# Norm sums from GpSimd to VectorE, and the root of the FFN norm at a fixed place among TensorE's products

## The chip, the cores and the metric

One core of a Trainium2 chip runs the whole kernel in one launch. The metric is the device time of an execution in microseconds (us). TensorE is called PE in the profile, its weight loads PEld, VectorE DVE, ScalarE ACT, GpSimd POOL, and SP the queue that issues most loads.

## The reference

A decoder trunk of two layers on x of 256 positions and 1024 features, in float32. Each layer is x = x + attention(rmsnorm(x)) @ w_o, then x = x + conv_ffn(rmsnorm(x)); a last rmsnorm follows. What matters here is the norm and the FFN:

```python
def rmsnorm(x, g):
    y = x * lax.rsqrt(jnp.mean(x * x, axis=-1, keepdims=True) + RMS_EPS)
    return y * g

def conv_ffn(h, w_up, conv_w, conv_b, w_down):      # h 256x1024, w_up 1024x5632, w_down 2816x1024
    u = h @ w_up
    up = jnp.pad(u, ((0, 0), (2, 0), (0, 0)))
    c = conv_b
    for j in range(3):
        c = c + conv_w[j] * up[:, j:j + S]
    val, gate = jnp.split(c, 2, axis=-1)
    return (jax.nn.silu(gate) * val) @ w_down
```

The attention of layer 0 has MoBA and indexer-selected heads, that of layer 1 sixteen dilated-window heads; their projections take the normed x too.

## The kernel before, in words

x is held transposed in xT: 128 partitions of features by 8 blocks k by 256 positions. Every float32 product is made of three products of rounded parts (mm3, line 125): a factor is split into a high part h (ScalarE copy to the rounded type) and a low part l (the difference, on VectorE), and h*h, h*l and l*h are added up in PSUM. Weights are split so by split (line 114), x by split_x (line 201) into xh and xl with the norm's gain g in it. The factor 1/rms of a position isn't needed before the products: it is multiplied in when the result leaves PSUM (in the FFN the tile rb at line 517; in layer 1's projections q_evac, k_evac and r at line 312).

The norm is built by the class Norm (line 208). At the end of an output projection (out_proj, line 413) or of FFN 0 (line 549) TensorE finishes the sum of x in four quarters b, each two blocks k. For each, take adds it to xT on VectorE (line 219), measure squares it on ScalarE (line 227, tile sq) and split_x makes two xh and two xl. In measure the squares of the quarters are added on GpSimd: two additions of 128x512 for b = 1 and 2, and 128x256 ones for b = 2 and 3. After the fourth, two products with a column of ones (line 239, tile sp) sum over the partitions, rsqrt_mean (line 174) makes the mean on VectorE and the power -0.5 on GpSimd, and row_bcast (line 181) spreads the root over the partitions: the root's two parts are multiplied into diagonals (tile d) on VectorE, two products with ones give the tile bp, and ScalarE copies it to rb. All of measure has high priority with the planner.

The FFN (ffn, line 471) runs over 22 steps f. A step loads columns of w_up (a load serves two steps; three buffers raw), splits the value half i = 0 and the gate half i = 1, and makes 24 products for each into one PSUM tile; the tile's tag goes lg, pt, lg, av from step to step, and sp and bp use av too. Then the result is multiplied by rb (u), convolved (c), gated (sg) and split into g. The down products of a step are made three steps later (LAG). The order of an engine's instructions is set when the program is built, by a planner that simulates the engines and takes, of what is ready, the earliest traced or the one with high priority. `behind(gate)` and `tc.issue_after` queue an instruction behind a named one on its engine; `pin` (`tc.keep_in_program_order`) queues it behind the one traced just before it on its engine. The splits of steps 1 to 3 are queued behind the norm's last xh and xl (norm.gate).

In FFN 1 the planner also places 16 transposes of xT to the token layout on TensorE (line 544) and four copies of them on VectorE (line 545). In layer 1 the low part of the first split of the k projection, k_0l, is made on GpSimd (line 758).

Of the kernel before, what the change touches and what calls it, by code (L numbers as in the profile page):

```python
# [34 lines left out]
def trunk(ctx, tc, x, w_in_even, idx_k_norm, w_in_odd, w_o, rel_bias, attn_norm, ffn_norm,  # L35
# [78 lines left out]
    def split(view, shape, name, gate=None, low=nc.vector):  # L114
        with behind(gate):
            return split_now(view, shape, name, low)

    def split_now(view, shape, name, low):
        h = wp.tile([P] + shape, F32R, tag="wh", name=name + "h", bufs=5)
        l = wp.tile([P] + shape, F32R, tag="wl", name=name + "l", bufs=5)  # L120
        nc.scalar.activation(h, view, AF.Copy)  # L121
        low.tensor_tensor(l, view, h.bitcast(F32), ALU.subtract)
        return h, l
# [11 lines left out]

    gps = lg_tile("gps")
# [37 lines left out]
    def rsqrt_mean(ss, n, name, w=2):  # L174
        var = tp.tile([P, w], F32, tag="var", name=name + "v")
        nc.vector.tensor_scalar(var, ss, 1.0 / n, EPS, op0=ALU.mult, op1=ALU.add)
        r = tp.tile([P, w], F32, tag="rstd", name=name + "r")
        nc.gpsimd.tensor_tensor(r, var, mhalf[:, 0:w], ALU.pow)
        return r

    def row_bcast(r, name):
# [5 lines left out]
        ps = av_tile(name + "bp")  # L187
        for i, part in enumerate((rh.bitcast(F32), rl)):
            for t in range(2):
                nc.vector.tensor_scalar(dg[:, i, t, :], ident, part[:, t:t + 1], None, op0=ALU.mult)  # L190
            nc.tensor.matmul(ps[:, 0:S], ones_r, dg[:, i, :, :].rearrange("p t c -> p (t c)"),
                             start=i == 0, stop=i == 1)
        rb = tp.tile([P, S], F32, tag="rb", name=name + "b")
        nc.scalar.activation(rb, ps[:, 0:S], AF.Copy)
        return rb

# [11 lines left out]
    class Norm:  # L208


        def __init__(self, grow, name):
            self.grow, self.name = grow, name

        def take(self, b, acc):
# [10 lines left out]
        def measure(self, b, xv):  # L225
            sq = tp.tile([P, 2, S], F32, tag=("c", "c", "u", "c")[b], name=f"{self.name}sq{b}", bufs=(3, 3, 2, 3)[b])
            nc.scalar.activation(sq, xv, AF.Square)
# [6 lines left out]
            self.sq = sq  # L234
            if b < 3:
                return
# [7 lines left out]
    pin = tc.keep_in_program_order  # L244
# [45 lines left out]
    def proj_fm(w2d, c0, xh, xl, evac, name, gate=(None, None), low=(nc.vector, nc.vector)):  # L290
        raw = load_cols(w2d, c0, name)
        ps = acc_tile(f"{name}p")
        for i in range(2):
            h, l = split(raw[:, :, i * P:(i + 1) * P], [8, P], f"{name}_{i}", gate[i], low[i])
# [176 lines left out]
    def ffn(layer, norm, name, nxt, also=None):  # L471
# [22 lines left out]
        def up(f, raws):  # L494
            ps = rot[f % 4](f"{name}u{f}")
            hl = [split(raws[i][:, :, (f % 2) * P:(f % 2 + 1) * P], [8, P], f"{name}w{f}_{i}",
                        norm.gate if 1 <= f < 4 else None) for i in range(2)]
# [312 lines left out]
```

## Time and profile before

| | us |
|---|---|
| median of 3 runs | 653.55 |
| lowest and highest | 653.11, 653.69 |
| the profiled execution | 653.59 |
| its span | 651.8 |
| PE busy in it | 637.5 |
| DVE busy | 529.9 |
| ACT busy | 406.0 |
| POOL busy | 58.7 |

The span runs from the first to the last instruction on the core; 1.8 us of the profiled execution lie around it. The granted clock was 0.998 of full speed over the span. A timeline line gives start, duration, engine, line of the kernel, operation, out<-in, and in brackets how long the engine had been idle and what released it. Lines of equal kind that follow each other are merged (x4), and their duration runs from the first start to the last end. Names leave out numbers: f0u is any step's result in FFN 0, f0w_0h the high part of its value half's weights.

### The profile page before, as it was taken

The page shows a single profiled execution, that of the slowest core. Times are in us where ns is not written, and L with a number is a line of the kernel's source. Part 1 is how long each engine was busy: PE and PEld are TensorE (multiplying, and loading weights), DVE is VectorE, ACT ScalarE, POOL GpSimd, SP SyncE. Part 2 cuts the span into 40 slices and gives each one's busy share as a digit, 9 for nine tenths or more (in the row PEclk, how much of TensorE's full clock was granted, in tenths as well). Part 3 has the DMA queues.
Part 4 walks back from the last instruction along what each step waited for, and adds up shares of the span by engine and source line. Part 5 has one row for each costly group of instructions (what it writes and reads, how often), then busy time and mean ns, then how long its engine had stood idle before and what let it go on. Part 6 is the DMA issues. An engine that isn't in the chain of part 4 may idle for free.

```text
span 651.8 us, 12933 instructions
## 1 busy us (share of the span) xinstructions
PE 637.5 (98%) x5145; PEld 612.5 (94%) x5145; DVE 529.9 (81%) x1012; ACT 406.0 (62%) x710; POOL 58.7 (9%) x68
## 2 busy tenths in 40 slices
PE   8999999999999999999999999999999999999995
PEld 6999999998999999999989999999999999999994
DVE  6999999968898778877779977865899877777774
ACT  6766775765766555555546866855486555555553
POOL 0100002803000000000013111000300000000002
PEclk9999999999999999999999999999999999999999
DMA  9987645462767666666424533637456655555201
GB/s 276 294 238 189 190 130 194 169 220 90 235 212 220 203 207 211 211 210 210 130 66 133 192 129 132 240 96 247 155 189 222 210 183 183 184 180 185 91 1 64
DMA packets 91604, 116.01 MB, mean 178 GB/s; under 512 B 3447, under 2 KB 83191, under 8 KB 91544
## 3 DMA queue, kind: packets, MB, share of 16 engines
q1 hardware_dynamic: 86492, 110.09, 51.5%
q10 hardware_dynamic: 5052, 5.10, 3.5%
q8 instruction: 40, 0.66, 0.4%
q14 instruction: 20, 0.16, 0.1%
HBM read 113.35 MB, written 1.84 MB: 177 GB/s over the span
## 4 chain that ended last, share of the span: by engine, by line
PE 94%; DVE 3%; DMA 1%; issue 1%; ACT 0%; SPq 0%; POOL 0%; POOLq 0%; DVEq 0%
PE f0u L130 19%; PE f1u L130 19%; PE f1o L130 9%; PE f0o L130 9%; PE a1o L130 3%; PE a0o L130 3%; PE a_0pt L386 1%; PE a1av L395 1%; PE a0av L395 1%; DVE xT L219 1%; PE v12p L130 1%; PE qi1p L130 1%; PE q00p L130 1%; PE v01p L130 1%; PE qi2p L130 1%; PE q12p L130 1%
## 5 line engine op out<-in xcount | busy, mean ns | idle before, releaser
L130 PE MATMUL f0u<-f0xl,f0w_0h 128*128 128x256 f32 x176 | 49.5, 281 | 1.2 <-DVE f0xl L204 1.2
L130 PE MATMUL f1u<-f1xl,f1w_0h 128*128 128x256 f32 x176 | 49.6, 282 | 0.7 <-DVE f1xl L204 0.7
L130 PE MATMUL f0u<-f0xh,f0w_0l 128*128 128x256 f32 x176 | 49.2, 280 | 0.0
L130 PE MATMUL f1u<-f1xl,f1w_1h 128*128 128x256 f32 x176 | 49.2, 280 | 0.0
L130 PE MATMUL f1u<-f1xh,f1w_0l 128*128 128x256 f32 x176 | 49.2, 279 | 0.0
L130 PE MATMUL f1u<-f1xh,f1w_1h 128*128 128x256 f32 x176 | 49.1, 279 | 0.0
L130 PE MATMUL f0u<-f0xl,f0w_1h 128*128 128x256 f32 x176 | 49.1, 279 | 0.0
L130 PE MATMUL f0u<-f0xh,f0w_1l 128*128 128x256 f32 x176 | 49.1, 279 | 0.0
L130 PE MATMUL f0u<-f0xh,f0w_1h 128*128 128x256 f32 x176 | 49.1, 279 | 0.0
L130 PE MATMUL f0u<-f0xh,f0w_0h 128*128 128x256 f32 x176 | 49.1, 279 | 0.0
L130 PE MATMUL f1u<-f1xh,f1w_1l 128*128 128x256 f32 x176 | 49.1, 279 | 0.0
L130 PE MATMUL f1u<-f1xh,f1w_0h 128*128 128x256 f32 x176 | 49.1, 280 | 0.0
L524 DVE SCALAR_TENSOR_TENSOR f1c<-f1us,cv,f1c 128x255 f32<-128x255 f32 (+1 forms) x88 | 36.9, 479 | 0.7 <-ACT f1c L521 0.7
L121 ACT ACTIVATE f1w_0h<-f1uv 128x1024 fp32r<-128x1024 f32 x22 | 23.2, 1056 | 22.2 <-PE f1u L130 20.4
L524 DVE SCALAR_TENSOR_TENSOR f0c<-f0us,cv,f0c 128x255 f32<-128x255 f32 (+1 forms) x88 | 36.9, 477 | 0.0
L121 ACT ACTIVATE f0w_0h<-f0uv 128x1024 fp32r<-128x1024 f32 x22 | 23.3, 1058 | 21.5 <-PE f0u L130 21.5
L130 PEld LDWEIGHTS f1u<-f1xl,f1w_0h 128*128 128x128 f32 x176 | 33.1, 188 | 1.9 <-DVE f1xl L204 1.1
L130 PEld LDWEIGHTS f0u<-f0xl,f0w_0h 128*128 128x128 f32 x176 | 33.1, 188 | 1.8 <-DVE f0xl L204 1.8
L121 ACT ACTIVATE f0w_1h<-f0ug 128x1024 fp32r<-128x1024 f32 x22 | 23.3, 1060 | 17.5 <-PE f0o L130 12.2
L121 ACT ACTIVATE f1w_1h<-f1ug 128x1024 fp32r<-128x1024 f32 x22 | 23.3, 1060 | 16.8 <-PE f1o L130 8.9
L130 PEld LDWEIGHTS f1u<-f1xh,f1w_0h 128*128 128x128 f32 x176 | 33.0, 188 | 0.8
L130 PEld LDWEIGHTS f1u<-f1xh,f1w_0l 128*128 128x128 f32 x176 | 33.1, 188 | 0.0
(1047 smaller groups left out, 2492.3 us busy)
## 6 DMA issues: line engine op xcount, KB each, us to landing
f0dn<-in_w_down_dram SPq DMA_DIRECT2D x11, 1024.0 KB, 4.9
f0uv<-in_w_up_dram SPq DMA_DIRECT2D x11, 1024.0 KB, 6.3
f0ug<-in_w_up_dram SPq DMA_DIRECT2D x11, 1024.0 KB, 6.3
f1dn<-in_w_down_dram SPq DMA_DIRECT2D x11, 1024.0 KB, 5.0
f1uv<-in_w_up_dram SPq DMA_DIRECT2D x11, 1024.0 KB, 6.8
f1ug<-in_w_up_dram SPq DMA_DIRECT2D x11, 1024.0 KB, 5.2
q<-in_w_in_even_dram SPq DMA_DIRECT2D x4, 1024.0 KB, 6.7
k<-in_w_in_even_dram SPq DMA_DIRECT2D x4, 1024.0 KB, 5.9
```

The source lines that it names most:

```text
L121: nc.scalar.activation(h, view, AF.Copy)
L130: m = nc.tensor.matmul(ps, w, a, start=start and i == 0, stop=stop and i == 2, **kw)
L219: nc.vector.tensor_tensor(xv[:, i, :], acc[:, i * S:(i + 1) * S], xv[:, i, :], ALU.add)
L386: m = nc.tensor.transpose(pt[:, c * P:(c + 1) * P], pr[:, c * P:(c + 1) * P], ident)
L395: m = nc.tensor.matmul(o[s * HD:(s + 1) * HD], V[:, t, vc], pts[s][:, qc], start=t == 0, stop=t == 1)
L524: nc.vector.scalar_tensor_tensor(c[:, i, sh:S], u[:, i, 0:S - sh], cv[:, j, col:col + 1], c[:, i, sh:S], op0=ALU.mult, op1=ALU.add)
```

## The change

The additions of the squares leave measure. take keeps the four tiles of squares, and after the fourth quarter sums makes four additions on VectorE, queued behind the last xl and with high priority: a += b, c += d, a += c (128x512 each) and the two halves of a (128x256). The second of them is called half, the fourth sum.

In the FFN the first three steps' products are traced before step 0's result is evacuated. The root (sp, mean, power) is pinned on TensorE between the value half and the gate half of step 1. The diagonals are traced in step 2, and the products that spread the root (over_rows) are pinned between the halves of step 2. On VectorE the low parts of the splits are queued: step 1's two behind half and behind sum, step 2's behind the mean and behind the last diagonal, step 3's behind the last diagonal; their high parts on ScalarE stay behind the last xh.

Layer 1's norm n1 has the same four sums on VectorE, and its root and broadcast are traced by the new measure after the FFN, with high priority as before. The argument low goes away: k_0l is made on VectorE, and k_0's two parts are queued behind the high and low part of the last g of FFN 0.

```diff
-    def split(view, shape, name, gate=None, low=nc.vector):
+    def split(view, shape, name, gate=None):
...
-        low.tensor_tensor(l, view, h.bitcast(F32), ALU.subtract)
+            nc.vector.tensor_tensor(l, view, h.bitcast(F32), ALU.subtract)
...
+            sq = tp.tile([P, 2, S], F32, tag=("c", "c", "u", "c")[b], name=f"{self.name}sq{b}", bufs=(3, 3, 2, 3)[b])
             with tc.high_priority():
-                self.measure(b, xv)
+                nc.scalar.activation(sq, xv, AF.Square)
+            self.sq.append(sq)
             for k in (2 * b, 2 * b + 1):
                 self.gate = split_x(self.xh, self.xl, self.grow, k)
...
-            if b in (1, 2):
-                nc.gpsimd.tensor_tensor(sq, sq, self.sq, ALU.add)
-            if b >= 2:
-                nc.gpsimd.tensor_tensor(sq[:, 0, :], sq[:, 0, :], sq[:, 1, :], ALU.add)
             if b == 3:
-                nc.gpsimd.tensor_tensor(sq[:, 0, :], sq[:, 0, :], self.sq[:, 0, :], ALU.add)
+                self.sums()
+
+        def sums(self):
+
+            a, b, c, d = self.sq
+            with tc.high_priority(), tc.issue_after(self.gate[1].ins):
+                nc.vector.tensor_tensor(a, a, b, ALU.add)
+                self.half = nc.vector.tensor_tensor(c, c, d, ALU.add)
+                nc.vector.tensor_tensor(a, a, c, ALU.add)
+                self.sum = nc.vector.tensor_tensor(a[:, 0, :], a[:, 0, :], a[:, 1, :], ALU.add)
+
+        def root(self, first=lambda m: m):
             ps = av_tile(self.name + "sp")
             for t in range(2):
-                nc.tensor.matmul(ps[:, t:t + 1], sq[:, 0, t * P:(t + 1) * P], ones[:, 0:1], start=True, stop=True)
-            self.r = rsqrt_mean(ps[:, 0:2], D, self.name)
-            self.rb = row_bcast(self.r, self.name)
+                first(nc.tensor.matmul(ps[:, t:t + 1], self.sq[0][:, 0, t * P:(t + 1) * P], ones[:, 0:1],
+                                       start=True, stop=True))
+            self.r, self.mean = rsqrt_mean(ps[:, 0:2], D, self.name)
+
+        def measure(self):
+            with tc.high_priority():
+                self.root()
+                self.rb = row_bcast(self.r, self.name)
...
+            def part(i, behind=None):
+                return split(raws[i][:, :, (f % 2) * P:(f % 2 + 1) * P], [8, P], f"{name}w{f}_{i}",
+                             behind and (norm.gate[0], behind))
+
+            ps = rot[f % 4](f"{name}u{f}")
+            if f == 1:
+                hl = [part(0, norm.half), part(1, norm.sum)]
+            elif f == 2:
+                hl = [part(0, norm.mean)]
+                dg, last_dg = row_diagonals(norm.r, norm.name)
+                hl.append(part(1, last_dg))
+                norm.last = last_dg
+            else:
+                hl = [part(i, norm.last if f == 3 else None) for i in range(2)]
...
+                    if i == 0 and f == 1:
+                        norm.root(pin)
+                    if i == 0 and f == 2:
+                        norm.rb = over_rows(dg, norm.name, pin)
+            return ps
+
+        raws = None
+        ups = [up(f) for f in range(3)]
+        rbb = norm.rb[:, None, :].to_broadcast([P, 2, S])
+        for f in range(NF):
+            ps = ups[f] if f < 3 else up(f)
...
         if not last:
+            nxt.behind = (high, low)
...
+    n1.measure()
     r1, rb1 = n1.r, n1.rb
...
-        gate, low = (n1.gate, nc.gpsimd) if c == 0 else (None, nc.vector)
+        gate, early = (n1.gate, n1.behind) if c == 0 else (None, None)
...
-                (None, gate), (low, nc.vector))
+                (early, gate))
```

## Rows read from the trace of the kernel before

**Rows 1.** The page's first part: busy time, share of the span and instructions of each engine.

```profile
PE 637.5 (98%) x5145; PEld 612.5 (94%) x5145; DVE 529.9 (81%) x1012; ACT 406.0 (62%) x710; POOL 58.7 (9%) x68
```

**Rows 2.** Windows. Columns: the stretch, its length, then busy time and instructions of PE, PEld, DVE, ACT and POOL, granted clock, DMA share, GB/s; a window counts an instruction that reaches into it from the stretch before. First the steady stretch of FFN 0; then its first step's products alone (tile f0u: PE, PEld, DVE); the hold in FFN 0's last products; the first q and the first k projection of layer 1 alone (tiles q10p, k10p); FFN 1's first step, its products alone (line 130: PE, PEld) and its transposes alone (line 544).

```profile
170.00:335.00 165.00, 165.00 (x1417) 165.00 (x1416) 136.06 (x213) 98.54 (x147) 0.00 (x0) 1.00 0.60 192
...
153.65:157.80 4.15, 2.92 (x18) 2.34 (x19) 0.00 (x0) 1.00 0.00 0
...
337.74:339.56 1.82, 0.28 (x3) 0.07 (x2) 1.76 (x1) 0.00 (x0) 1.48 (x1) 1.00 1.05 366
...
343.05:349.86 6.81, 4.71 (x25) 3.50 (x25) 0.00 (x0) 1.00 0.01 2
...
343.05:349.86 6.81, 4.10 (x22) 3.29 (x22) 0.00 (x0) 1.00 0.01 2
...
456.12:461.38 5.26, 3.59 (x21) 2.58 (x20) 1.00 0.25 100
...
456.12:461.38 5.26, 2.67 (x16) 1.86 (x16) 1.00 0.25 100
```

**Rows 3.** The waits of PE: instruction that waited, releaser, us in total, times, longest.

```profile
PE f0o L130 <- DVE f0g L534: 1.5, 1, 1.5
...
PE f0u L130 <- DVE f0xl L204: 1.2, 2, 0.8
...
PE q10p L130 <- DVE n1xl L204: 0.7, 2, 0.4
```

**Rows 4.** Timeline of POOL and then of DVE at FFN 0's norm.

```profile
152.96 2.71 POOL L229 TENSOR_TENSOR f0sq<-f0sq,f0sq 128x512 f32<-128x512 f32 x2 [21.73 <-ACT f0sq L227]
...
152.07 0.48 DVE L204 SCALAR_TENSOR_TENSOR f0xl<-xT,gT,f0xh 128x256 fp32r<-128x256 f32 x1
...
153.24 2.71 DVE L204 SCALAR_TENSOR_TENSOR f0xl<-xT,gT,f0xh 128x256 fp32r<-128x256 f32 x2
155.87 0.74 DVE L219 TENSOR_TENSOR xT<-a0o,xT 128x256 f32<-128x256 f32 x2
156.54 2.14 DVE L204 SCALAR_TENSOR_TENSOR f0xl<-xT,gT,f0xh 128x256 fp32r<-128x256 f32 x4
```

**Rows 5.** Timeline of ACT at the same norm: a square, then the high parts of x.

```profile
153.59 0.62 ACT L227 ACTIVATE f0sq<-xT 128x512 f32<-128x512 f32 x1
154.11 0.49 ACT L203 ACTIVATE f0xh<-xT,gT 128x256 fp32r<-128x256 f32 x1
156.32 0.51 ACT L203 ACTIVATE f0xh<-xT,gT 128x256 fp32r<-128x256 f32 x1 [1.71 <-DVE xT L219]
```

**Rows 6.** Timeline from FFN 0's last g to layer 1's norm: DVE, ACT and POOL.

```profile
335.16 0.42 DVE L528 TENSOR_TENSOR f0sg<-f0sg,f0c 128x256 f32<-128x256 f32 x1
337.12 2.38 DVE L534 TENSOR_TENSOR f0g<-f0sg,f0g 128x256 fp32r<-128x256 f32 x1 [1.54 <-ACT f0g L531]
340.45 1.46 DVE L219 TENSOR_TENSOR xT<-f0o,xT 128x256 f32<-128x256 f32 x4 [0.94 <-PE f0o L130]
...
345.58 3.89 DVE L204 SCALAR_TENSOR_TENSOR n1xl<-xT,gT,n1xh 128x256 fp32r<-128x256 f32 x5
...
336.69 0.40 ACT L531 ACTIVATE f0g<-f0sg 128x256 fp32r<-128x256 f32 x1
...
336.86 2.36 POOL L122 TENSOR_TENSOR k_0l<-k,k_0h 128x1024 fp32r<-128x1024 f32 x1 [172.82 <-ACT k_0h L121]
343.41 2.72 POOL L229 TENSOR_TENSOR n1sq<-n1sq,n1sq 128x512 f32<-128x512 f32 x2 [4.18 <-ACT n1sq L227]
```

**Rows 7.** Timeline of DVE at FFN 1's norm: low parts of x, and the first copy to the token layout.

```profile
455.71 2.79 DVE L204 SCALAR_TENSOR_TENSOR f1xl<-xT,gT,f1xh 128x256 fp32r<-128x256 f32 x2
...
459.48 0.68 DVE L545 COPY f1xtok<-f1xt 128x512 f32<-128x512 f32 x1
460.08 1.78 DVE L204 SCALAR_TENSOR_TENSOR f1xl<-xT,gT,f1xh 128x256 fp32r<-128x256 f32 x2
```

**Rows 8.** Groups of DVE by shape in 170 to 335 us: busy us, mean ns, then idle time before.

```profile
L122 DVE TENSOR_TENSOR f0w_1l<-f0ug,f0w_1h 128x1024 fp32r<-128x1024 f32 x19 | 23.2, 1223 | 0.4 <-ACT f0w_1h L121 0.4
...
L534 DVE TENSOR_TENSOR f0g<-f0sg,f0g 128x256 fp32r<-128x256 f32 x21 | 8.8, 420 | 0.0
```

**Rows 9.** Timeline of the root in FFN 0: PE, POOL and DVE (f0rl reads f0rh; the diagonals f0d are the last).

```profile
161.54 0.50 PE L239 MATMUL f0sp<-ones,f0sq 128*128 128x1 f32 x4
...
163.34 0.70 POOL L178 TENSOR_TENSOR f0r<-f0v,mhalf 128x2 f32<-128x2 f32 x1 [2.37 <-DVE f0v L176]
...
164.07 0.17 DVE L183 CAST f0rh<-f0r 128x2 fp32r<-128x2 f32 x1 [0.81 <-POOL f0r L178]
164.28 0.16 DVE L185 TENSOR_TENSOR f0rl<-f0r,f0rh 128x2 f32<-128x2 f32 x1
...
164.75 0.48 DVE L190 TENSOR_SCALAR f0d<-ident,f0rl 128x128 fp32r<-128x128 f32 x2
```

**Rows 10.** Timeline of SP's queue and of ACT: the load of step 2's gate columns and the split that takes it.

```profile
160.40 0.37 SPq L94 DMA_DIRECT2D f0ug<-in_w_up_dram  x1
...
165.56 1.06 ACT L121 ACTIVATE f0w_1h<-f0ug 128x1024 fp32r<-128x1024 f32 x1 [4.97 <-DMA f0ug<-in_w_up_dram]
```

**Rows 11.** Timeline of DVE and PE at the first down products of FFN 0.

```profile
181.29 0.41 DVE L534 TENSOR_TENSOR f0g<-f0sg,f0g 128x256 fp32r<-128x256 f32 x1
...
181.52 0.63 PE L130 MATMUL f0o<-f0g,f0d0h 128*128 128x256 f32 x4
```

More of the change, by code (lines that the diff above doesn't have):

```diff
@@ L112, in behind @@
             yield
-    def split(view, shape, name, gate=None, low=nc.vector):
+    def split(view, shape, name, gate=None):
         with behind(gate):
[L116 to L121, printed above, removed]
-        low.tensor_tensor(l, view, h.bitcast(F32), ALU.subtract)
+            h = wp.tile([P] + shape, F32R, tag="wh", name=name + "h", bufs=5)
+            l = wp.tile([P] + shape, F32R, tag="wl", name=name + "l", bufs=5)
+            nc.scalar.activation(h, view, AF.Copy)
+            nc.vector.tensor_tensor(l, view, h.bitcast(F32), ALU.subtract)
         return h, l
@@ L133, in mm3 @@
         return m.ins
+    pin = tc.keep_in_program_order
     gps = lg_tile("gps")
@@ L186, in row_bcast, with over_rows @@
         dg = tp.tile([P, 2, 2, P], F32R, tag="dg", name=name + "d", bufs=1)
-        ps = av_tile(name + "bp")
         for i, part in enumerate((rh.bitcast(F32), rl)):
             for t in range(2):
-                nc.vector.tensor_scalar(dg[:, i, t, :], ident, part[:, t:t + 1], None, op0=ALU.mult)
-            nc.tensor.matmul(ps[:, 0:S], ones_r, dg[:, i, :, :].rearrange("p t c -> p (t c)"),
-                             start=i == 0, stop=i == 1)
+                m = nc.vector.tensor_scalar(dg[:, i, t, :], ident, part[:, t:t + 1], None, op0=ALU.mult)
+        return dg, m
+    def over_rows(dg, name, first=lambda m: m):
+        ps = av_tile(name + "bp")
+        for i in range(2):
+            first(nc.tensor.matmul(ps[:, 0:S], ones_r, dg[:, i, :, :].rearrange("p t c -> p (t c)"),
+                                   start=i == 0, stop=i == 1))
         rb = tp.tile([P, S], F32, tag="rb", name=name + "b")
@@ L195, in row_bcast @@
         return rb
+    def row_bcast(r, name):
+        return over_rows(row_diagonals(r, name)[0], name)
     def norm_tiles(name):
@@ L211, in __init__ @@
         def __init__(self, grow, name):
-            self.grow, self.name = grow, name
+            self.grow, self.name, self.sq = grow, name, []
         def take(self, b, acc):
@@ L286, in trunk, with proj_fm @@
                                          start=n + k + i == 0, stop=n == 2 and k == KT - 1, skip_group_check=True))
-    def proj_fm(w2d, c0, xh, xl, evac, name, gate=(None, None), low=(nc.vector, nc.vector)):
+    def proj_fm(w2d, c0, xh, xl, evac, name, gate=(None, None)):
         raw = load_cols(w2d, c0, name)
@@ L293, in proj_fm @@
         for i in range(2):
-            h, l = split(raw[:, :, i * P:(i + 1) * P], [8, P], f"{name}_{i}", gate[i], low[i])
+            h, l = split(raw[:, :, i * P:(i + 1) * P], [8, P], f"{name}_{i}", gate[i])
             for k in range(KT):
@@ L492, in down, with up @@
                         down_tok(f, t, c, h, l, gh, gl)
[L494 to L497, printed above, removed]
-            for ks in (range(0, 6), range(6, 8)) if f == 0 else (range(8),):
-                for i in range(2):
-                    h, l = hl[i]
-                    for k in ks:
-                        mm3(ps[:, i * S:(i + 1) * S], h[:, k, :], l[:, k, :], xh[:, k, :], xl[:, k, :],
-                            k == 0 and i == 0, k == KT - 1, skip_group_check=True)
-            return ps
-        rbb = norm.rb[:, None, :].to_broadcast([P, 2, S])
-        for f in range(NF):
+        def up(f):
+            nonlocal raws
             if f % 2 == 0:
@@ L514, in ffn @@
                     dn.append(raw_dn[:, i, :])
-            ps = up(f, raws)
+            def part(i, behind=None):
[11 more added lines that the diff above has]
+                hl = [part(i, norm.last if f == 3 else None) for i in range(2)]
+            for ks in (range(0, 6), range(6, 8)) if f == 0 else (range(8),):
+                for i in range(2):
+                    h, l = hl[i]
+                    for k in ks:
+                        mm3(ps[:, i * S:(i + 1) * S], h[:, k, :], l[:, k, :], xh[:, k, :], xl[:, k, :],
+                            k == 0 and i == 0, k == KT - 1, skip_group_check=True)
+                    if i == 0 and f == 1:
[8 more added lines that the diff above has]
+            ps = ups[f] if f < 3 else up(f)
             u = tp.tile([P, 2, S], F32, tag="u", name=f"{name}us{f}")
@@ L533, in ffn @@
                 also(f, high.ins)
-            nc.vector.tensor_tensor(gl, sg, gh.bitcast(F32), ALU.subtract)
+            low = nc.vector.tensor_tensor(gl, sg, gh.bitcast(F32), ALU.subtract)
             pend.append((f, gh, gl))
@@ L602, in trunk @@
         nc.vector.tensor_add(ss0s, ss0[:, :, 0], ss0[:, :, 1])
[L603 removed]
+        r0, _ = rsqrt_mean(ss0s, D, "n0")
     kiw = cp.tile([80, S], F32, tag="kiw", name="kiw")
```

16 lines of the change are left out of this document (4 added, 12 removed).

## The prediction

> **What bounds the kernel now.** The order in which I read: the busy shares, the windows of TensorE, its waits, then the timelines of the other engines where it waits. TensorE is busy for 98% of the span [rows 1]. In the long steady stretch of the first FFN it does 1417 products in 165.00 us, 0.1164 us each, without a gap [rows 2]; there nothing but its own work counts, and neither VectorE's 81% nor ScalarE's 62% is a bound. So the change can bring only what TensorE loses at the three norms. The PE waits name the culprit each time as VectorE: the low halves of x (f0xl, n1xl), and once the low half of the last gated value (f0g) [rows 3].
>
> How much is lost is read from stretches against that pace [rows 2]. First step of FFN 0: 18 products take 4.15 us in place of 2.10, loss 2.05. The hold inside f0's last products: 1.82 us for one product, loss 1.70. First step of layer 1's projections: 24 + 22 products (the 25th of the q row begins at the window's end) take 6.81 in place of 5.36, loss 1.45. First step of FFN 1: 18 products (2.10) and 16 transposes, whose weight loads take 1.86 together, fill 3.96 of 5.26, loss 1.30; the loads overlap, so it may be more, and I take 1.40. All four: 6.60 us.
>
> Why is VectorE late? One f0xl takes 0.48 us, but two of them, begun just after GpSimd began its pair of 128x512 additions, take 2.71, and four more take 2.14 under the next ones [rows 4]. The same in layer 1 (three n1xl and two more: 5 in 3.89 against GpSimd's 343.41 onward) and in FFN 1 (2.79 for two, 1.78 for two [rows 6, 7]). And f0g's low half, 0.42 us by its 21 sisters [rows 8], takes 2.38 while GpSimd makes k_0l from 336.86 [rows 6]. Each stretched instruction reads two SBUF operands beside a GpSimd instruction that reads SBUF.
>
> **The change, part by part.** *Removed from GpSimd:* per norm the 128x512 and 128x256 additions, and once the subtraction k_0l. With them the stretching goes, and what TensorE then waits for is ScalarE's and VectorE's plain chain. For FFN 0: two x additions of about 0.42 take 0.74 [rows 4], so queued independent instructions overlap by some 0.08, and one adds 0.40 for an f0xl. VectorE does two f0xl from 153.24 in 0.8 and the last quarter's two x additions in 0.67, so f0xl 4 and 5 end near 155.2 and 155.6. TensorE wants them at 153.65 + 13 x 0.1164 = 155.2 and 155.5. Loss left: about 0.15 of 2.05. ScalarE is no later than that: its xh 5 runs at 154.11, and only the late addition kept xh 6 until 156.32 [rows 5]; two xh of 0.4 and a square of 0.5 by their starts, so from 154.5 it needs 0.4 + 0.5 + 0.5, so xh 7 ends near 156.0 and f0xl 7 near 156.4. In layer 1 f0g's low half comes within 0.5 us of its high half, which need no longer stand behind k_0h (the multiply ends 335.6, f0g high began only at 336.69 [rows 6]); TensorE reaches it at 337.86, so all 1.70 come back. The x chain of that norm starts 1.7 earlier than 340.45 [rows 6], with ScalarE's 1.3 us per quarter as above; the 12 products per quarter of two interleaved projections take 1.4, so nothing is left of the 1.45. In FFN 1 I leave 0.05.
>
> *Added to VectorE:* four sums behind the last xl. No row has a 128x512 addition of two SBUF operands; the neighbours are 0.42 for 128x256 and 1.22 for 128x1024 [rows 8], between them 0.69. A dependent instruction starts 0.21 after one of 0.17 [rows 9], so it waits for the end; an independent one overlaps by 0.08. Sum: 0.61 + 0.73 + 0.73 + 0.34 = 2.4 us. The Trainium skill speaks against such a chain (VectorE: DVE Perf Modes, "The TRN2 errata"): SBUF latency is paid between instructions, and an fp32 tensor_tensor of N elements takes (N+151) cycles at 0.96 GHz. That is an estimate of 2.5 us for the four; by it the sum below would change by 0.05. The trace agrees at both ends (0.42 and 1.22 are what it gives).
>
> What the sums delay is the second step's first split, f1w_0l in FFN 0. Its products begin at 153.65 + 48 x 0.1164 + 0.15 = 159.4 and want the low half 0.23 later. If the planner lets the split in right behind the second sum, it ends at 156.4 + 1.2 + 1.2 = 158.8 and nothing waits; if all four sums (they have high priority) come first, it ends at 160.0 and TensorE waits 0.4. The code allows both; I take the middle, 0.2. In FFN 1 the sixteen transposes give TensorE 1.8 us of other work, but four copies of 0.6 us to the token layout run on VectorE (0.68 with its tail [rows 7]); with two of them ahead of the sums the split ends between 462.7 and 463.8, wanted at 463.6: I take 0.1, and 1.2 if all four copies go first. In layer 1 the splits k_1, v_0, v_1 stand behind the sums, but are wanted only 8.4 us after the start; k_0l, 1.2 us on VectorE after f0g's low half, fits into the 2.2 us from 336.5 to the first x addition, 338.75. Cost 0; if that cover were gone, each would cost its 1.2 or 2.4.
>
> *Moved:* the root. Its two products stand pinned between the halves of step 2, the broadcast between the halves of step 3. They are the same instructions as before (4 passes from 161.54 [rows 9]), so TensorE's work is unchanged. From the root's products the mean is there some 0.7 us later, then the split f2w_0l queued behind it (1.2), GpSimd's power (0.70 [rows 9]), six small VectorE instructions (164.07 to 165.23, 1.2 [rows 9]): the broadcast's diagonals are ready some 3.9 us after the root, and TensorE asks for them 0.36 + 2.8 + 2.8 = 6.0 us after it. f2w_0l itself is wanted at 3.4 and ready at 2.0, or 2.7 if the power stretches it. Cover 0.7 at the least. The Trainium skill (SBUF — State Buffer, "Who interferes with whom") says that of two such instructions the later one blocks for the whole of the other. By that the power and f2w_0l now meet in each FFN where before VectorE stood idle; the stall would be one of the two numbers just used, and both stay inside the cover.
>
> *Queues:* SP's next weight load waits for step 2's first split to free its buffer (issued 160.40, and ScalarE takes it at 165.56 after 4.97 idle [rows 10]). It now goes out near 159.4 and lands near 164.6; its split is done by 167.5, TensorE wants it near 168.7. It moves with the rest, cover about 1 us. In FFN 1 it is the same with about 1 us.
>
> *Later evacuation:* the broadcast now comes at the middle of step 3 of TensorE, so step 1's result is evacuated at about the same absolute time as before while TensorE is 2 us further on. It has three PSUM tiles free of that (steps 2 to 4) and the down products only join when g is there: f0d0's first at 181.52 beside g's low half of 181.29 [rows 11], in the middle of step 5. I cost it at nothing, the cover being steps 4 and 5.
>
> Sum: 6.60 - 0.15 - 0.2 - 0.05 - 0.1 = 6.1 us. The profiled execution took 653.59 us (span 651.8, 1.8 around it, unchanged), 0.04 above the median 653.55: 653.6 - 6.1 = **647.5 us**.
>
> **Rivals.**
> *The sums become the last wait.* The planner puts all sums and FFN 1's copies ahead of the splits: 0.4 in FFN 0, 1.2 in FFN 1 and some of the x chain (0.5) again: 648.6 to 650.5, likeliest 649. For it: high priority on the sums; against it: the split may follow the second sum.
> *The planner's order changes elsewhere.* Layer 1's attention fills TensorE without loss now, so a new order there can only lose; one wait of 0.5 per head pair over eight pairs would be 4: 650.5 to 652.
> *It doesn't do what it says.* If f0xl were long for another reason than GpSimd, only the hold of 1.70 comes back: 651.9; with the sums in the chain ahead of the splits (0.4 to 1.2 twice), up to 653.5. Against it: the same instruction takes 0.48 with GpSimd idle [rows 4].
> *Slower.* The later evacuation decides: if the planner puts f0d0's products right behind step 4 (ending near 176.7) while g is not there before 181, TensorE's queue stands for up to 4.3 us in each FFN: 653.6 - 6.1 + 8.6 = 656. It turns slower once each hold is over 3.05 us. Against it: the planner now waits with d0 until g is there, to 0.2 us [rows 11].
>
> **How the numbers follow.** Forecast (646.2 to 648.6) 0.62; sums last 0.18; order elsewhere 0.08; not as said 0.06, a third of it under 652.2; slower 0.06. The low end is all 6.60 back and 0.8 for unread small waits and spread. The range 646.2 to 650.5 takes in the forecast and the sums' case, 0.80. A measurement of this kernel tells 0.2%, 1.3 us, from no change: faster 0.90, same 0.04, slower 0.06.
>
> **What would show it.** Right: no 128x512 addition on GpSimd; every f0xl, n1xl and f1xl near 0.48; f0g's low half 0.42 and no PE wait on it; the first 18 products of FFN 0 in 2.1 to 2.3 us; f0sp and f0bp without a wait ahead of them. Wrong: xl still stretched; a PE wait on the low half of step 2's split over 1 us; a PE wait on f0g ahead of d0; PE waits in the a1 head pairs.

## The result, and the profile after

The changed kernel took 647.5 us (median of 4 runs, 646.88 to 647.92) where the kernel before took 653.62 (4 runs); the ratio is 0.9903, 95% interval 0.9885 to 0.992, that is 6.3 us less (5.2 to 7.5). The forecast was 647.5. The profiled execution took 646.88, its span is 645.1, against 653.59 and 651.8. The times in this document are of the faster of two states that executions show; one execution of e12, 894.19 us at a granted clock of 0.655, is left out for that.

The page's first part, kernel after [rows 1]:

```profile
PE 636.1 (99%) x5145; PEld 612.2 (95%) x5145; DVE 528.2 (82%) x1025; ACT 405.8 (63%) x710; POOL 41.7 (6%) x52
```

TensorE has as many instructions as before. The span is 6.7 us shorter: 5.3 of it is idle time of TensorE that is gone (14.3 us before, 9.0 now), and 1.4 is busy time, for the profile counts part of a held-up product as busy (18 products of FFN 0's first step were 2.92 us busy before, where the pace makes 2.10). The kernel before has two more waits than its rows 3 show:

```profile
PE f1u L130 <- DVE f1xl L204: 0.7, 1, 0.7
...
PE a1o L130 <- ACT a1mxh L398: 0.5, 1, 0.5
```

All of TensorE's waits in the kernel after [rows 3]:

```profile
PE warm_ps L87 <- DVE warm L84: 1.3, 1, 1.3
```

That one is the start-up. The waits on f0g, f0xl, n1xl and f1xl are all gone, and so is the one on a1mxh. Why, one reads at FFN 0's norm, timeline of DVE (L210 makes xl, L239 to L242 the four sums, L119 a split's low half) [rows 4]:

```profile
152.58 0.88 DVE L210 SCALAR_TENSOR_TENSOR f0xl<-xT,gT,f0xh 128x256 fp32r<-128x256 f32 x2
...
154.04 1.76 DVE L210 SCALAR_TENSOR_TENSOR f0xl<-xT,gT,f0xh 128x256 fp32r<-128x256 f32 x4
155.71 0.69 DVE L239 TENSOR_TENSOR f0sq<-f0sq,f0sq 128x512 f32<-128x512 f32 x1
156.31 0.69 DVE L240 TENSOR_TENSOR f0sq<-f0sq,f0sq 128x512 f32<-128x512 f32 x1
156.92 1.22 DVE L119 TENSOR_TENSOR f0w_0l<-f0uv,f0w_0h 128x1024 fp32r<-128x1024 f32 x1
158.05 0.69 DVE L241 TENSOR_TENSOR f0sq<-f0sq,f0sq 128x512 f32<-128x512 f32 x1
158.77 0.43 DVE L242 TENSOR_TENSOR f0sq<-f0sq 128x256 f32<-128x256 f32 x1
```

A pair of f0xl takes 0.88 where it took 2.71, four take 1.76 where they took 2.14; each of the 24 xl of the three norms takes 0.47 to 0.48 us. The sums take 2.4 us behind them, and here the planner put the second step's first split between the second and the third sum. At the end of FFN 0, DVE [rows 6]:

```profile
333.51 0.42 DVE L566 TENSOR_TENSOR f0g<-f0sg,f0g 128x256 fp32r<-128x256 f32 x1 [0.48 <-ACT f0g L563]
334.46 1.23 DVE L119 TENSOR_TENSOR k_0l<-k,k_0h 128x1024 fp32r<-128x1024 f32 x1 [0.53 <-ACT k_0h L118]
...
340.32 2.15 DVE L210 SCALAR_TENSOR_TENSOR n1xl<-xT,gT,n1xh 128x256 fp32r<-128x256 f32 x5
```

f0g's low half 0.42 for 2.38, five n1xl 2.15 for 3.89, and k_0l on VectorE is done before the first addition to x at 336.09.

Two windows of TensorE, the first step of FFN 0 up to its second half's first product and the first step of FFN 1 (length, PE busy, granted clock, DMA share, GB/s) [rows 2]:

```profile
152.99:155.31 2.32, 2.32 (x21) 1.00 0.00 0
...
449.95:453.84 3.89, 3.89 (x36) 1.00 0.41 135
```

Where the time came from, by the first product of each stage (timelines of PE):

| stage, from first product to first product | before | after | difference |
|---|---|---|---|
| start to FFN 0 (untouched code) | 153.65 | 152.99 | -0.66 |
| FFN 0 to layer 1's projections | 189.40 | 185.70 | -3.70 |
| layer 1's projections to FFN 1 | 113.07 | 111.26 | -1.81 |
| FFN 1 to its last product's end | 188.88 | 187.51 | -1.37 |
| from there to the end of the span (untouched) | 6.8 | 7.64 | +0.84 |

The three stages that the change touches give 6.88. The two ends are no part of it, and they nearly cancel (the last section says more of them). The ends move from execution to execution by more than many of the differences below, so beside each median the length of the stages is worth reading; a table at the end of the experiments has it for every run.

### The profile page after: what moved, and what is told of

Read it like the earlier page. It is cut to its first block, busy times and chain, and to the rows that moved or that the text cites. A ratio compares the mean times of both kernels' runs of the same rounds, so it can differ in the third digit from the quotient of the medians.

```text
span 645.1 us, 12921 instructions
## 1 busy us (share of the span) xinstructions
PE 636.1 (99%) x5145; PEld 612.2 (95%) x5145; DVE 528.2 (82%) x1025; ACT 405.8 (63%) x710; POOL 41.7 (6%) x52
## 4 chain that ended last, share of the span: by engine, by line
PE 98%; DMA 1%; DVE 0%; POOL 0%; SPq 0%; issue 0%; POOLq 0%
PE f0u L127 19%; PE f1u L127 19%; PE f0o L127 10%; PE f1o L127 9%; PE a1o L127 4%; PE a0o L127 4%; PE a_0pt L398 1%; PE a1av L407 1%; PE a0av L407 1%; PE qi0p L297 1%; PE v13p L127 1%; PE qi1p L127 1%; PE v10p L127 1%; PE k11p L127 1%; PE q00p L127 1%; PE v11p L127 1%
## 5 line engine op out<-in xcount | busy, mean ns | idle before, releaser
L556 DVE SCALAR_TENSOR_TENSOR f0c<-f0us,cv,f0c 128x254 f32<-128x254 f32 (+1 forms) x88 | 37.2, 479 | 0.1
L127 PEld LDWEIGHTS f1u<-f1xh,f1w_1h 128*128 128x128 f32 x176 | 33.1, 188 | 0.1
```

The source lines that it names most:

```text
L127: m = nc.tensor.matmul(ps, w, a, start=start and i == 0, stop=stop and i == 2, **kw)
L556: nc.vector.scalar_tensor_tensor(c[:, i, sh:S], u[:, i, 0:S - sh], cv[:, j, col:col + 1], c[:, i, sh:S], op0=ALU.mult, op1=ALU.add)
```

## The experiments

The expectations count a step as the code does, by f: their step 1 (f = 1) is the prediction's second step, their step 3 (f = 3) its fourth.

**e1: the subtraction k_0l alone.** The kernel before, with this and nothing else:

```diff
-            nc.vector.tensor_tensor(gl, sg, gh.bitcast(F32), ALU.subtract)
+            low = nc.vector.tensor_tensor(gl, sg, gh.bitcast(F32), ALU.subtract)
...
+            nxt.behind = (high, low)
...
-        gate, low = (n1.gate, nc.gpsimd) if c == 0 else (None, nc.vector)
+        gate, early = (n1.gate, n1.behind) if c == 0 else (None, None)
...
-                (None, gate), (low, nc.vector))
+                (early, gate))
```

> One part alone: only k_0l goes from GpSimd to VectorE, behind the last g. Theory (a GpSimd instruction that reads SBUF holds up a VectorE instruction with two SBUF operands): f0g's last low half goes from 2.38 to 0.42 us, TensorE's wait on it of 1.5 us is gone, x's low halves stay as long as before; 653.6 - 1.7 = 651.9. Rival (the order of VectorE's and ScalarE's queues is what counts): k_0l now stands ahead of the x additions and takes back what it gives, 653 or more.

Measured 652.0 us (651.53 to 653.41), ratio 0.9968 (0.9958 to 0.9979). TensorE's wait on f0g is gone, its waits on f0xl (1.2), n1xl (0.8) and f1xl (0.7) are within 0.1 of those before. This part is worth 1.7 by the medians and 1.8 by the length of FFN 0's stage.

**e3: the other way round**, the changed kernel with k_0l back on GpSimd.

```diff
...
-        gate, early = (n1.gate, n1.behind) if c == 0 else (None, None)
+        gate, low = (n1.gate, nc.gpsimd) if c == 0 else (None, nc.vector)
...
-                (early, gate))
+                (None, gate), (low, nc.vector))
```

> The changed kernel with k_0l back on GpSimd, in the place it had. Theory: f0g's low half is 2.4 us long again and TensorE waits 1.5 for it, 647.5 + 1.7 = 649.2. Rival (order): no wait of TensorE there, 647.5 within 0.7.

Measured 649.51 us, ratio 0.9935 (0.9921 to 0.9948). The wait of 1.5 on f0g is back and no other. So k_0l is worth about the same whichever engine has the sums: 2.0 by the medians here and 1.7 in e1, 1.8 by FFN 0's stage in both.

**e2: the four sums alone.** The kernel before, its additions on VectorE behind the last xl; the root, its broadcast and the splits are where the planner wants them.

```diff
-                nc.gpsimd.tensor_tensor(sq, sq, self.sq, ALU.add)
...
+            with tc.issue_after(self.gate[1].ins):
+                nc.vector.tensor_tensor(a, a, b, ALU.add)
+                nc.vector.tensor_tensor(c, c, d, ALU.add)
+                nc.vector.tensor_tensor(a, a, c, ALU.add)
+                nc.vector.tensor_tensor(a[:, 0, :], a[:, 0, :], a[:, 1, :], ALU.add)
```

> The other part alone: the four sums on VectorE behind the last low half of x; root, broadcast and splits planned freely as before, k_0l still on GpSimd. Theory: the three first steps get back what they got in the changed kernel (1.8, 1.45 and 1.4, together 4.6 us), the hold at f0g stays: 649.0. Rival (the fixed places of root and splits do it): the sums' 2.4 us on VectorE stand ahead of splits or of the root, and no more than half comes back, 651.3 or more.

Measured 658.99 us, ratio 1.0071 (1.005 to 1.0091): slower than before, by 4.6 us of 653.7 (3.3 to 5.9). My theory that the sums' engine is the whole of it falls here. Half of it stands: layer 1's stage, where nothing of the FFN's root stands in the way, is 111.26 us long, as in the changed kernel. The loss lies in the two FFN, where e2 has the waits that the next run shows, and in FFN 1 the granted clock is 0.50 from 480 to 484 us.

**e7: the sums and k_0l together, still without the fixed places.** The edits of e1 and e2 in one kernel; beside the lines of e2:

```diff
...
-                (None, gate), (low, nc.vector))
+                (early, gate))
```

> Both parts without the fixed places (no pinned root, steps 1 to 3 traced as before, splits behind the last x halves only). Theory: 647.5, as the changed kernel, within 0.7. Rival: the fixed places are worth at least 1.5 us, 649 or more, with TensorE waiting on a split or on the evacuation in steps 1 to 5.

Measured 655.81 us, ratio 1.0031 (1.0015 to 1.0048): 8.3 above the changed kernel, which has the same sums on the same engine. The xl are as short as there (f0xl 0.87 for two). Its waits of PE:

```profile
PE f1u L130 <- ACT f1b L194: 1.9, 1, 1.9
PE f0u L130 <- ACT f0b L194: 1.9, 1, 1.9
...
PE f1bp L191 <- DVE f1d L190: 1.1, 1, 1.1
PE f0bp L191 <- DVE f0d L190: 0.4, 1, 0.4
```

TensorE now waits for the root's broadcast (bp) and for its evacuation (f0b). Timelines of DVE and ACT of e7 (L236 the fourth sum, L176 the mean, L190 the diagonals, L121 and L122 a split's high and low half):

```profile
161.31 0.42 DVE L236 TENSOR_TENSOR f0sq<-f0sq 128x256 f32<-128x256 f32 x1
164.77 1.23 DVE L122 TENSOR_TENSOR f0w_1l<-f0ug,f0w_1h 128x1024 fp32r<-128x1024 f32 x1 [3.04 <-ACT f0w_1h L121]
165.91 0.15 DVE L176 TENSOR_SCALAR f0v<-f0sp 128x2 f32<-128x2 f32 x1
...
171.05 0.48 DVE L190 TENSOR_SCALAR f0d<-ident,f0rl 128x128 fp32r<-128x128 f32 x2
...
163.68 1.06 ACT L121 ACTIVATE f0w_1h<-f0ug 128x1024 fp32r<-128x1024 f32 x1 [5.16 <-DMA f0ug<-in_w_up_dram]
...
172.46 1.06 ACT L121 ACTIVATE f0w_1h<-f0ug 128x1024 fp32r<-128x1024 f32 x1 [3.21 <-DMA f0ug<-in_w_up_dram]
173.43 0.37 ACT L194 ACTIVATE f0b<-f0bp 128x256 f32<-128x256 f32 x1
```

Read the brackets. The sum is done at 161.7, but VectorE stands 3.04 us in front of the low half of a split whose high half waits for its load on ScalarE, with the mean behind it; the last diagonals come at 171.05 (164.95 in the changed kernel). Then ScalarE stands in front of a split of a later step, which waits 3.21 us for its load, with the evacuation f0b behind it, and TensorE's products of f = 3 want the PSUM tile that f0b empties.

In FFN 1 the pause brings one thing more. Windows of PE in e7 (length, PE busy, granted clock, DMA share, GB/s):

```profile
472.00:474.00 2.00, 0.92 (x6) 1.00 1.07 365
474.00:476.00 2.00, 0.08 (x2) 0.96 1.02 329
476.00:478.00 2.00, 2.00 (x9) 0.50 0.46 152
478.00:480.00 2.00, 2.00 (x14) 0.69 0.00 0
480.00:482.00 2.00, 2.00 (x19) 1.00 0.00 0
```

After 3.0 us of waits within 4 the granted clock is 0.50, the lower of its two levels (1.2 GHz), until about 479.2: 9 products in 2 us where 19 is the rule. That adds 1.6. FFN 0's stage is 2.9 longer than in the changed kernel, 2.3 of it waits; FFN 1's is 5.0 longer, 3.0 of it waits and 1.6 the lower clock. Layer 1's stage is the same, and the ends give back 0.4, so that the profiled executions lie 7.48 apart (654.36 and 646.88).

**e11: which part of the fixed places?** e7, with the splits of steps 1 to 3 held as in the changed kernel; the root's products go where the planner puts them.

```diff
...
+            held = {1: (norm.half, norm.sum), 2: (norm.mean, norm.last), 3: (norm.last, norm.last)}.get(f)
+            return held and (norm.gate[0], held[i])
```

> The kernel of e7 (four sums on DVE, k_0l on DVE, the root's products where the planner puts them, steps traced one by one) with one thing of the change more: the splits of steps 1 to 3 held behind the sums, the mean and the last diagonal, as in the changed kernel. Theory (what e7 lost is splits that stand ahead of the fourth sum and of the root's chain on DVE and ahead of the root's evacuation on ACT, one of which waits for its load): the waits of TensorE on the broadcast (0.4 and 1.1) and on its evacuation (1.9 and 1.9) go, the lower clock behind the second of them goes with it, and the time is that of the changed kernel, 647.5, within 0.7. Rival (the fixed places of the root's products on TensorE are what is needed): two of the waits or more stay, 650 or more.

Measured 646.79 us, ratio 0.9896 (0.9878 to 0.9915): the changed kernel's time. All four waits of e7 are gone, though the root's products stand elsewhere (the broadcast comes 4.9 us behind the root's sum on TensorE, 5.8 in the changed kernel). So the holds on the splits are what is needed, not the pins on TensorE and not the three steps traced ahead. The profiled execution is the slowest of the six, 649.41. Its layer 1 and FFN 1 are within 0.1 of the changed kernel's, its FFN 0 is 1.6 longer without a wait: there a step of 72 products takes 8.48 us in place of 8.40 throughout, at a granted clock of 1.00.

**e12: half of these holds**, only those of step 2's second split and step 3's two.

```diff
-            held = {1: (norm.half, norm.sum), 2: (norm.mean, norm.last), 3: (norm.last, norm.last)}.get(f)
+            held = {1: (norm.gate[1], norm.gate[1]), 2: (norm.gate[1], norm.last), 3: (norm.last, norm.last)}.get(f)
```

> The kernel of e11 with half of the gates: step 2's second split and step 3's two behind the last diagonal, but step 1's splits and step 2's first one free behind the last part of x, so that two of them can stand ahead of the fourth sum. It tells apart where e7's splits do their harm. If ahead of the evacuation (the queue behind the last diagonal, with the split that waits for its load): 648, at most one wait of under 0.5 in each FFN. If already ahead of the fourth sum: the sum is 1.2 to 2.4 later than in the changed kernel, the broadcast with it, the wait of step 3 on the evacuation stays at 1 to 1.9 in each FFN, and the time is 650 to 653.

Measured 647.79 us (647.39 to 650.39), ratio 0.9912 (0.9892 to 0.9931). Two splits stand ahead of the fourth sum again and the root's products come at 164.63, as late as in e7, but TensorE doesn't wait for the root or its evacuation. By their stages FFN 0 is 0.4 and FFN 1 0.9 longer than in the changed kernel. The one wait of PE on that way is on a split that the late root holds back in FFN 1:

```profile
PE f1u L130 <- DVE f1w_1l L122: 0.4, 1, 0.4
```

So most of the harm in e7 is done behind the fourth sum, by splits ahead of the mean, the diagonals and the evacuation, two of which wait for their load. Which of these places costs most is open: the two holds of e12 clear them together.

**e8: the fixed places alone**, the sums back on GpSimd, k_0l on VectorE.

```diff
...
+            if b in (1, 2):
+                nc.gpsimd.tensor_tensor(sq, sq, self.sq[0], ALU.add)
...
-                self.sums()
...
-                hl = [part(0, norm.half), part(1, norm.sum)]
+                hl = [part(0, norm.gate[1]), part(1, norm.gate[1])]
```

> The changed kernel with its sums back on GpSimd in the form of the kernel before; the root's products and the splits of steps 2 and 3 stay in their fixed places, step 1's splits behind the last part of x, k_0l stays on DVE. Theory (the fixed places earn nothing by themselves: before, TensorE waited neither for the root nor for its broadcast): the stretched xl and their waits come back, 1.8 + 1.3 + 1.4 above the changed kernel, 652.0, which is the time of the kernel with k_0l alone moved. Rival (the fixed places are worth something of their own): 651 or less.

Measured 653.48 us, ratio 0.9996 (0.9985 to 1.0007). The waits on f0xl (1.2), n1xl (0.8) and f1xl (0.7) are those of e1, and the fixed places earn nothing, as the theory said; but the time is 1.5 above e1, which it didn't say. In the profiled execution (655.52) the waits on f0xl are followed by the lower clock, windows of PE:

```profile
154.00:158.00 4.00, 2.76 (x19) 1.00 0.00 0
158.00:162.00 4.00, 4.00 (x23) 0.57 0.03 6
162.00:166.00 4.00, 4.00 (x35) 1.00 0.99 326
```

That is 12 products fewer in 4 us, 1.4 us. In this execution too a later step of FFN 0 takes 8.48 us for 8.40, which makes 1.6 more; layer 1 and FFN 1 are as long as in e1. The 1.5 of the median is another matter. Six of the twelve executions have a granted clock of 0.998 or more over the span, too high for such a stretch at 0.50, and their median is 653.3. So the lower clock doesn't set it; what does is open, since these executions have no rows.

**e5: is it GpSimd beside the xl?** The changed kernel with additions on GpSimd that nobody needs.

```diff
...
+                    for _ in range(3):
+                        nc.gpsimd.tensor_tensor(lb, flat, flat, ALU.add)
```

> The changed kernel with three GpSimd additions more in each norm, 128x384 each, that read the second quarter's squares as soon as they are made and write a tile that nothing reads: work added, nothing of the result changed, and every instruction of the other engines stands in the order of the changed kernel. Theory (a GpSimd addition beside an xl stretches the xl, whatever order the planner makes): some 3 us of additions, where the kernel before had 5.4 beside its first xl of FFN0, which cost 1.8 there; so about 1 in each of the three stages comes back, xl of 1 us and more in place of 0.44, and waits of TensorE on xl: 649.5 to 651. Rival (it was the sums' place in the planner's order that cost the time, not the two engines side by side): xl as before, 647.5 within 0.7.

Measured 649.46 us, ratio 0.9936 (0.9924 to 0.9948). Timelines of POOL and DVE of e5:

```profile
153.09 2.76 POOL L234 TENSOR_TENSOR f0lb<-f0sq 128x384 f32<-128x384 f32 x3 [21.72 <-ACT f0sq L228]
...
153.37 1.80 DVE L210 SCALAR_TENSOR_TENSOR f0xl<-xT,gT,f0xh 128x256 fp32r<-128x256 f32 x2
155.09 0.74 DVE L225 TENSOR_TENSOR xT<-a0o,xT 128x256 f32<-128x256 f32 x2
155.75 1.73 DVE L210 SCALAR_TENSOR_TENSOR f0xl<-xT,gT,f0xh 128x256 fp32r<-128x256 f32 x4
```

The pair of xl beside the additions takes 1.80 for 0.88; the four behind them 1.73, as in the changed kernel. The stages are longer by 1.0, 0.8 and 0.7, a wait on f0xl is back (0.4), and in FFN 1 TensorE waits 0.5 for the second step's first split. The order of the instructions on TensorE, VectorE and ScalarE is that of the changed kernel, so it is the two engines side by side.

**e6: GpSimd that only writes.**

```diff
...
+                with tc.high_priority(), tc.issue_after(done.ins):
+                    for _ in range(12):
+                        pin(nc.gpsimd.memset(lb, 0.5))
```

> The same place and order, but with twelve GpSimd memsets of 128x384 in each norm in place of the additions: GpSimd as busy (12 by 0.42, 5.0 us) over all the xl, but it reads nothing of SBUF. If it is GpSimd's reading that gets in the way of the xl, which read two tiles of SBUF: xl at 0.44, no wait, 647.5 within 0.7. If any GpSimd access to SBUF does: xl at 0.8 to 1.5 and 1.5 to 2 in each stage, 652 or more.

Measured 648.72 us, ratio 0.9924 (0.9911 to 0.9937); but the memsets of FFN 0 ran at 134.3 to 139.6, before the norm, and those of the other two norms at 165.3 and 430.5, long before theirs: holding an instruction behind one of another engine made no wait here. So the run decides nothing of the xl. It shows something else. The memsets meant for layer 1's norm fell on FFN 0's root, timelines of POOL and DVE of e6:

```profile
165.35 5.74 POOL L234 MEMSET n1lb<- 128x384 f32 x12
...
165.45 0.35 DVE L182 CAST f0rh<-f0r 128x2 fp32r<-128x2 f32 x1 [0.60 <-POOL f0r L176]
...
165.91 0.49 DVE L188 TENSOR_SCALAR f0d<-ident,f0rh 128x128 fp32r<-128x128 f32 x2
166.33 0.58 DVE L188 TENSOR_SCALAR f0d<-ident,f0rl 128x128 fp32r<-128x128 f32 x2
166.83 1.21 DVE L119 TENSOR_TENSOR f0w_1l<-f0ug,f0w_1h 128x1024 fp32r<-128x1024 f32 x1
```

In the changed kernel the copy f0rh takes 0.17 and the second pair of diagonals 0.47. So beside GpSimd instructions that only write, these took longer, while the split behind them, with two operands from SBUF, took its usual 1.21. FFN 0's stage is 0.9 longer, with a wait of 0.5 on f0g.

**e13: the memsets in their place.**

```diff
...
+                    pin(nc.gpsimd.tensor_tensor(lb[:, 0:2], sq[:, 0, 0:2], sq[:, 0, 0:2], ALU.add))
+                    for _ in range(9):
+                        pin(nc.gpsimd.memset(lb, 0.5))
```

> In e6 the memsets of FFN 0 ran at 134.3 to 139.6, long before the xl, so e6 says nothing of them. Here each norm's memsets (nine of 128x384, 0.42 each, 3.8 us in all) stand on GpSimd behind an addition of 128x2 that reads the second quarter's squares, so they run where e5's additions ran; the other engines keep the changed kernel's order. If it is GpSimd's reading of SBUF that stretches the xl: pairs of xl at 0.87, no wait on them, 647.5 within 0.7. If GpSimd's writing does too: pairs at 1.4 to 1.9 as in e5, 649.5 or more.

Measured 646.94 us, ratio 0.9903 (0.9887 to 0.992). Timelines of POOL and DVE of e13:

```profile
153.41 4.25 POOL L235 MEMSET f0lb<- 128x384 f32 x9
...
153.42 0.87 DVE L210 SCALAR_TENSOR_TENSOR f0xl<-xT,gT,f0xh 128x256 fp32r<-128x256 f32 x2
...
154.88 1.76 DVE L210 SCALAR_TENSOR_TENSOR f0xl<-xT,gT,f0xh 128x256 fp32r<-128x256 f32 x4
```

GpSimd is busy beside all six xl, longer than in e5, and they take what they take alone; so it is in the other two norms, and the three stages are as long as in the changed kernel within 0.1. The order on TensorE, VectorE and ScalarE is again the same. So GpSimd's reading is what stretches the xl. The Trainium skill (SBUF — State Buffer, "Who interferes with whom") states this: a VectorE instruction with two SBUF inputs contends with a GpSimd instruction that reads SBUF, not with one that only writes it. e5 and e13 agree.

**e14: the changed kernel again**, beside e13.

> The changed kernel once more, on the chip and in the rounds of the kernel with the placed memsets, so that the two can be set side by side: 647.5 within 0.7.

Measured 648.1 us (647.43 to 648.85), ratio 0.9917 (0.9902 to 0.9932), with no wait of PE but in the start-up. The first product of FFN 0 stands at 154.84 in its profiled execution, at 152.99 in the first one: the spread is in the start-up, and the three stages are the same within 0.05.

**e4: the room of step 1's first split.** The changed kernel with it behind the fourth sum.

```diff
...
-                hl = [part(0, norm.half), part(1, norm.sum)]
+                hl = [part(0, norm.sum), part(1, norm.sum)]
```

> The changed kernel with step 1's first split behind the fourth sum in place of the second: the sum is ready 1.2 earlier and the split 1.1 later. By the changed kernel's rows that split's product is due 0.9 after its end in FFN0 and 0.3 after it in FFN1, so TensorE waits about 0.1 and 0.7: 648.3, between 647.5 and 649. It tells how much room the place of that split has.

Measured 647.82 us, ratio 0.9911 (0.9896 to 0.9926). One wait of PE is new, in FFN 1:

```profile
PE f1u L127 <- DVE f1w_0l L119: 0.5, 1, 0.5
```

The wait is not all of it. By their stages FFN 0 is 0.34 and FFN 1 1.04 longer than in the changed kernel, 1.4 together, where 0.1 + 0.7 were expected. The medians (647.82 here, 647.5 and 648.1 for the changed kernel) don't tell that apart, for the ends of the executions differ by as much.

**All runs by stage**, from first product to first product in the profiled execution, us:

| run | FFN 0 | layer 1 | FFN 1 |
|---|---|---|---|
| before | 189.40 | 113.07 | 188.88 |
| changed | 185.70 | 111.26 | 187.51 |
| e14, changed again | 185.75 | 111.28 | 187.51 |
| e1, k_0l alone | 187.57 | 113.27 | 188.89 |
| e3, k_0l back | 187.51 | 111.26 | 187.51 |
| e2, sums alone | 190.30 | 111.26 | 193.90 |
| e7, sums and k_0l | 188.58 | 111.26 | 192.54 |
| e11, e7 with the holds | 187.33 | 111.35 | 187.48 |
| e12, half the holds | 186.07 | 111.28 | 188.45 |
| e8, places alone | 190.85 | 113.27 | 188.80 |
| e5, GpSimd reads | 186.72 | 112.03 | 188.24 |
| e6, GpSimd writes early | 186.56 | 111.25 | 187.51 |
| e13, GpSimd writes | 185.78 | 111.26 | 187.51 |
| e4, split behind the sums | 186.04 | 111.26 | 188.55 |

## Why the prediction was right, step by step

**The mechanism** (xl and f0g stretched by GpSimd): right, and shown by e1, e3, e5 and e13.

**The terms of the sum.** FFN 0's first step, 2.05 less 0.15: 1.83 came (4.15 to 2.32). The hold at f0g, 1.70: FFN 0's stage is 3.70 shorter, and e1 and e3 put the hold at 1.83 and 1.81 of it. Layer 1's first stretch, 1.45: the q and k products of the first halves took 6.81 and take 5.36 (338.69 to 344.05). FFN 1, 1.40 less 0.15: 1.37. So the wait of 0.2 and 0.1 that I put on the second step's split was not needed: I took the middle between two orders, and the planner made a good one. In FFN 0 the split stands right behind the second sum, in FFN 1 behind the second sum and all four copies (it begins at 456.17), and TensorE waits in neither. e4 shows the other end, which I had at 0.4 + 1.2: 0.34 + 1.04.

**The sums.** I put 2.4 us on the chain of four; they take 0.60 + 0.61 + 0.72 + 0.43 = 2.36. The 0.69 that I took between 0.42 and 1.22 is what one 128x512 addition takes. But two of my four terms were wrong and cancelled: the second sum needs nothing of the first and overlaps it (0.61, I had 0.73), and the fourth needs the third and waits for its end (0.43, I had 0.34).

**The root's chain.** Diagonals 3.9 us after the root's products: 161.84 to 165.42, 3.6; TensorE takes them at 167.65, 5.8 after, where I had 6.0. The power does meet the split f0w_0l, timelines of DVE and POOL of the changed kernel [rows 9]:

```profile
162.38 0.16 DVE L174 TENSOR_SCALAR f0v<-f0sp 128x2 f32<-128x2 f32 x1 [2.04 <-PE f0sp L247]
162.46 1.23 DVE L119 TENSOR_TENSOR f0w_0l<-f0uv,f0w_0h 128x1024 fp32r<-128x1024 f32 x1
...
162.62 1.63 POOL L176 TENSOR_TENSOR f0r<-f0v,mhalf 128x2 f32<-128x2 f32 x1 [31.90 <-DVE f0v L174]
```

0.70 before, 1.63 now: it ends 0.56 behind the split's end at 163.69. By the Trainium skill (SBUF — State Buffer, "Who interferes with whom") the later of two such instructions blocks for the whole of the other. The rows agree, with the power as the later one: it begins 0.16 behind the split and ends behind it. It stayed inside its cover, as forecast; in FFN 1 it is 1.55.

**The later evacuation**, costed at nothing: right for this kernel, f0d0's first product comes at 181.30 (181.52 before) without a wait. But why it costs nothing I told only in part. I weighed the fixed places as something that moves the root, and looked for their price. I didn't ask what the sums on VectorE would do without them. e2 and e7 answer: 4.6 and 2.0 us slower than before, by their ratios, since splits that the planner may place freely go ahead of the root's chain and of its evacuation, some before their load is there. The rival that I called slower (the evacuation decides, 656) has the time that e7 measures, 655.8, but that is chance: it comes by another queue than I had it. The products of f = 3 wait for the PSUM tile of the broadcast, not the down products for g, and a part of it is the lower clock, which I had nowhere. The holds on the splits are what keeps it off.

**The planner's order elsewhere** "can only lose": wrong in its sign. Layer 1 gained 1.81, not 1.45; the wait of 0.5 on a1mxh that the kernel before has in its second attention is gone. I had taken that stage for free of waits. That the new order of the sums removed this wait is not shown by a run of its own, but in the three kernels with the sums on GpSimd (before, e1, e8) the wait is there and the stage is 113.1 to 113.3 long, and in all others the wait is gone and the stage is 111.2 to 111.4, or 112.03 in e5 with its stretched xl. By stage the gain was 0.30 (FFN 0), 0.36 (layer 1) and 0.12 (FFN 1) over the forecast, 6.88 in place of 6.1. The tail took 0.84 of it back and the start-up gave 0.66, so that the profiled execution lies at 646.88. With e14 the changed kernel's medians are 647.5 and 648.1: that forecast and median agree to the tenth is luck.

## What to carry to other kernels

A small task on GpSimd that reads SBUF isn't free when VectorE does two-input work on the path at that time (2.71 us here for a pair that takes 0.88): look for instructions that take several times their sisters' duration, and for who runs beside them. But moving such a task to VectorE moves what depends on it, and where a planner orders the queues, splits or copies that wait for a load can slip in ahead of a short chain that TensorE needs; hold them behind the chain's last instruction, and measure the move both with and without the holds, for here the move alone was slower than doing nothing. A pause of TensorE can cost more than its length (in FFN 1 of e7 1.6 us more at the lower clock, in its FFN 0 none of that). And compare stages as well as whole times: the medians of e4 and of the changed kernel hide 1.4 us that the stages show.

## What the runs showed of the hardware that was not expected

The granted clock fell to 0.50 after waits of TensorE of 1.1 and 1.9 us in FFN 1 of e7 (0.92 and 0.08 us busy in the two windows of 2 us before), and to 0.50 after 0.8 and 0.4 in e8 (158.2 to 161.4); after 0.4 and 1.9 in FFN 0 of e7 it stayed at 1.00, and so it did in the profiled execution of the kernel before after the same waits on f0xl as in e8. Which pause brings it down isn't settled by these rows. The kernel before seems to meet it too. It was executed 54 times beside the experiments: 12 executions with a granted clock of 0.994 over the span took 654.57 to 655.62 us, the other 42, at 0.996 or more, 652.89 to 654.47. The low ones have no rows, so where their clock fell isn't shown. All eight executions of the changed kernel are at 0.996 or more.

The pace of the same products at a granted clock of 1.00 has two values here. A later step of FFN 0 (72 products) takes 8.48 us in the profiled executions of e8 and e11 and 8.40 in all others, and 8.40 in FFN 1 of these two as well. Over the stage that is 1.6 us. Why isn't settled.

A power of 128x2 on GpSimd takes 0.69 to 0.70 us alone and, over all runs, 1.53 to 1.63 where it begins beside a 128x1024 split on VectorE.

The untouched ends of the kernel differ as much as small edits do: FFN 0's first product lies at 152.99 and 154.84 in two profiled executions of the changed kernel, and from TensorE's last product to the span's end it is 7.6 and 7.7 in these two and 7.7 in e3, 7.0 in e4, 7.5 in e6, 6.8 in the kernel before and in e1, e2, e5, e7, e8, e11, e12 and e13. The rows of the engines behind the last product are the same, so the difference lies behind them, where only the output's transfers are left; why isn't settled.
